# A two-layer hybrid backbone: GpSimd's products, sums, differences and copies on VectorE

## The chip, the cores and the metric

One core of one Trainium2 chip. The time is device time in microseconds (us) of one launch of the whole program. The engines in the profile are PE (TensorE, matmuls), PEld (TensorE's weight loads), DVE (VectorE), ACT (ScalarE), POOL (GpSimd) and SP (SyncE, which here issues nearly all DMAs).

## The reference

Two layers. In each, a modulated RMSNorm feeds four token mixers in parallel (gated DeltaNet, S5, differential attention, gated linear attention); their outputs are merged by sigmoid gates, multiplied by `w_out` and added to the stream; a second norm feeds a router and a mixture of experts (16 experts, two per token). Layer 0 computes 768 tokens (256 of context, 512 latent), layer 1 only what the 512 latent tokens need.

```python
def merge_branches(a, ys, w_branch, w_gate, b_gate, w_out):
    acc = 0.0
    for i, y in enumerate(ys):
        gate = jax.nn.sigmoid(a @ w_gate[:, i * dm:(i + 1) * dm] + b_gate[i * dm:(i + 1) * dm])
        acc = acc + gate * (y.astype(a.dtype) @ w_branch[i])
    return acc @ w_out

def moe_ffn(h, w_router, b_router, w_e_gate, w_e_up, w_e_down):
    scores = jax.nn.sigmoid((h @ w_router).astype(F32))
    ...                       # two experts per token, tokens sorted into blocks of 128
    def expert_block(args):
        rows, e = args
        hid = jax.nn.silu(rows @ w_e_gate[e]) * (rows @ w_e_up[e])
        return hid @ w_e_down[e]
```

## The kernel before

Activations lie in SBUF with 128 channels or 128 tokens on the partitions. Every large fp32 product is made of three TensorE matmuls (`mm3`): each operand is split into a high part `hi` that TensorE's fp32r format holds exactly and a rest `lo = raw - hi`; the product is hi·hi + lo·hi + hi·lo. So each weight tile costs one DMA (`raw`, `wr`), one ScalarE copy that rounds (`hi`, `wh`) and one subtraction (`lo`, `wl`). `wunit` makes a split for projections, gates, merge and `w_out`; `unit` makes one for the experts (six tiles of 128x2048 per expert, j = 0 to 5: two of gate, up and down each).

The program order of a layer: norm and projections; the mixers (DeltaNet, linear attention, attention head by head, S5), while the gate matmuls `pg` (L1299 to L1301 with `ah` and `al`; 1536 in layer 0) fill TensorE's gaps; the tables of the next layer's S5 (`s5_tables`, lines 1030 to 1130, with the small matmuls `s_w` and `s_h`) at the end of layer 0's mixers; the merge (`pb`, then `t`, L1765 to L1772); the product with `w_out` (`po`), the second norm and the router; the routing (lines 1966 to 2165), which ends in `tokfirst`, the list of tokens of the first block; then the experts: `front` gathers a block's rows with an indirect DMA on GpSimd's queue (`x`, L2220), transposes them on TensorE (`pt`) and splits them (`xh`, `xl`); `gate_up` and `down` are matmuls `pg`, `ph`, `pd`; an indirect DMA scatters the result (L2264). After layer 1 the pairs are added and normed.

GpSimd makes a part of the elementwise work: the `wl` of every gate tile (`pool_lo=True`), one in three `lo` of the experts (j = 2 and 5; of each layer's first expert j = 0, 1, 2 and 5, `FIRST_LO`), three of the four adds per output block of the merge, half of the S5 tables, and products in the mixers and norms. The tile framework's scheduler simulates the program when it is built, and the order of instructions on each engine follows from that simulation. An engine runs its own list strictly in that order, and each instruction waits by semaphores for what it reads and overwrites. The experts' `raw` tiles lie in a ring, and a later tile is loaded when the `hi` and `lo` of an earlier one are done.

Of the kernel before, what the change touches and what calls it, by code (L numbers as in the profile page):

```python
# [7 lines left out]
F32 = mybir.dt.float32  # L8
# [3 lines left out]
OP = mybir.AluOpType  # L12
# [11 lines left out]
AFTER = (1, 2, 5)  # L24
# [13 lines left out]
FIRST_LO = (0, 1, 2, 5)  # L38
# [319 lines left out]
def dn_pair(K, l, pr, S, qT, kT, vT, o_out, need):  # L358
# [68 lines left out]
    for d, m in ((0, "mskf"), (1, "mskb")):  # L427
        nc.gpsimd.tensor_mul(Dm[:, 12 * d:12 * d + 12], Dm[:, 12 * d:12 * d + 12],
                             K.c(m)[:, None, :].to_broadcast([128, 12, 64]))
# [89 lines left out]
    for d in range(2):  # L519
        nc.gpsimd.tensor_mul(Rk[:, d], Kb, eG[:, pr, d].rearrange("p t h -> p (t h)")[:, :, None].to_broadcast([128, 12, 64]))  # L520
    for d in range(2):
        nc.gpsimd.tensor_mul(kd[:, d], Kb, wk[:, d].rearrange("p t h -> p (t h)")[:, :, None].to_broadcast([128, 12, 64]))
# [21 lines left out]
    nc.gpsimd.tensor_mul(Mt.rearrange("p s h e -> p (s h) e"), K.c("id64")[:, None, :].to_broadcast([128, 24, 64]),  # L544
# [45 lines left out]
    for h in range(2):  # L590
        nc.gpsimd.tensor_copy(qs[64 * h:64 * h + 64], qT[64 - 64 * h:128 - 64 * h])
    Ev = EG.rearrange("p (t h) i -> p t h i", h=2)
    for d in range(2):
        dr = slice(64 * d, 64 * d + 64)
        for h in range(2):
            for t0, t1 in ((0, 2), (2, 6)):
                if t0 >= T0:
                    c0 = tcol(t0)
                    q_ = (qT if d == h else qs)[dr, c0:c0 + (t1 - t0) * 128].rearrange("p (t i) -> p t i", i=128)
                    (nc.gpsimd if d else nc.vector).tensor_mul(Ev[dr, t0:t1, h], Ev[dr, t0:t1, h], q_)  # L600
# [42 lines left out]
def finish_heads(K, pool, tag, o, tiles, eps, gain, z=None, rq=None, sq=None, head=None):  # L643
# [20 lines left out]
    if z is None:  # L664
        nc.gpsimd.tensor_mul(ov, ov, gb)
        return
# [4 lines left out]
    nc.gpsimd.tensor_mul(th, th, gb)  # L671
# [15 lines left out]
def gla(K, l, qT, kT, lowT, vsrc, need):  # L687
# [56 lines left out]
    nc.gpsimd.tensor_mul(kd, bf, kT[:, None, :].to_broadcast([128, 2, 768]))  # L744
# [63 lines left out]
def diff_attn(K, l, qk, V, o, with_ctx, done):  # L808
# [16 lines left out]
    for t in range(2, NT):  # L825
# [11 lines left out]
    def prep(h, st):  # L837
# [3 lines left out]
        for i in range(4):  # L841
# [7 lines left out]
            nc.gpsimd.tensor_sub(lo, src, sp[:, a:, 0, :].bitcast(F32))  # L849
# [180 lines left out]
def s5_tables(K, l, P, h, td):  # L1030

    nc, p, I = K.nc, K.s5, K.I
    V, G = nc.vector, nc.gpsimd
# [41 lines left out]
    G.memset(Bd, 0.0)  # L1075
# [48 lines left out]
    G.memset(dec[:, :, :, 0:1], 0.0)  # L1124
# [10 lines left out]
def s5_half(K, l, td, h, ud, zd):  # L1135
# [3 lines left out]
    V, G = nc.vector, nc.gpsimd  # L1139
# [22 lines left out]
    for d in range(2):  # L1162
# [26 lines left out]
        G.memset(x[:, :, :, first:first + 1], 0.0)  # L1189
# [86 lines left out]
def wunit(K, ring, src, shape, bufs, raw_bufs=2, pool_lo=False, tag="w", scale=None, raw_tag=None):  # L1276
# [61 lines left out]
def norm_a(K, l, md, tile_of, ah, al):  # L1338
# [56 lines left out]
    def block(s, t0, t1, k):  # L1395
# [8 lines left out]
        (nc.vector if k % 3 == 2 else nc.gpsimd).tensor_sub(al[:, k, c], v[:, 0:n], ah[:, k, c].bitcast(F32))  # L1404
# [85 lines left out]
def mixers(K, l, md, hold, tile_of, yd, gd, tds):  # L1490
# [243 lines left out]
def merge(K, l, md, hsrc, yd, gd, h1d, fd, lg, R, side):  # L1734
# [15 lines left out]
    for oc in range(8):  # L1750
# [79 lines left out]
    def product(t):  # L1830
# [7 lines left out]
        for n in range(2):  # L1838
# [4 lines left out]
            (nc.gpsimd if n == 0 else nc.vector).tensor_add(h[:, cc], h[:, cc], u[:, cc])  # L1843
# [28 lines left out]
    def tails(ss, *ts):  # L1872
# [6 lines left out]
        for i, (t, h, ps) in enumerate(ts):  # L1879
            s = 1 if t < 2 else 0  # L1880
            a, b = h[:, 0:512], h[:, 512:D]
            if t < NT - 2:
                nc.scalar.activation(a, a, AF.Copy, scale=r[:, i:i + 1])
                nc.gpsimd.tensor_mul(a, a, rows["sc", s][:, 0:512])
            else:
                nc.vector.scalar_tensor_tensor(a, a, r[:, i:i + 1], rows["sc", s][:, 0:512], op0=OP.mult, op1=OP.mult)
            nc.gpsimd.tensor_add(a, a, rows["sh", s][:, 0:512])
# [76 lines left out]
def route(K, l, lg, R):  # L1964
# [16 lines left out]
    V, G = nc.vector, nc.gpsimd  # L1981
# [18 lines left out]
    G.memset(pre[:, 0], 0.0)  # L2000
# [128 lines left out]
    G.memset(R.ent, 0)  # L2129
# [39 lines left out]
def moe(K, l, fd, metad, R, pd, ra, na, routing, rest):  # L2169
# [21 lines left out]
    def unit(e, j, alone=False, pool_lo=None, after=None):  # L2191
# [12 lines left out]
        with tc.issue_after(after.ins) if after else contextlib.nullcontext():  # L2204
            (nc.gpsimd if (j % 3 == 2 if pool_lo is None else pool_lo) else nc.vector).tensor_sub(l_, r, h.bitcast(F32))  # L2205
        return hi, lo

    def front(c, src):
# [3 lines left out]
        else:  # L2212
# [3 lines left out]
            nc.gpsimd.tensor_scalar(wt, mt[:, 2:3].bitcast(F32), 0.5, None, op0=OP.mult)  # L2216
# [50 lines left out]
    def run(work, first=False):  # L2267
# [7 lines left out]
        for i, (e, ranked, _) in enumerate([(w[0], len(w) > 2, 0) for w in work]):  # L2275
            if ranked:
                e = nc.values_load(R.exps[0:1, e:e + 1], min_val=0, max_val=13, engines=[mybir.EngineType.SP])
            us = [unit(e, j, pool_lo=j in FIRST_LO if first and i == 0 else None,
                       after=gathers[0] if first and i == 0 and j in AFTER else None, **kw) for j in range(4)]
            nxt = [front(*x) for x in work[i + 1][1]] if i + 1 < len(work) else None  # L2280
            hds = gate_up(frs, us)
            us = [unit(e, j, pool_lo=j in FIRST_LO if first and i == 0 else None,
                       after=gathers[0] if first and i == 0 and j in AFTER else None, **kw) for j in range(4, 6)]
# [32 lines left out]
def combine(K, l, md, p, h, t, rows, pd):  # L2316
# [7 lines left out]
    for i, e in ((0, nc.gpsimd), (1, nc.vector)):  # L2324
# [147 lines left out]
```

## Time and profile before

| | |
|---|---|
| time, median of 3 runs | 2811.99 us (2797.94 to 2814.32) |
| profiled execution | 2812.61 us, span of the trace 2810.6 us |
| PE busy | 2443.4 us (87%) |
| DVE busy | 1870.6 us (67%), 3515 instructions |
| ACT busy | 1218.6 us (43%) |
| POOL busy | 1178.3 us (42%), 854 instructions |
| DMA | 534.95 MB, mean 190 GB/s |
| mean granted TensorE clock | 0.908 |

The span is one launch on the core, 2 us less than the time of the same execution. A busy share is a share of the span; the engines work beside each other, so the shares don't add up to one.

### The profile page before, as it was taken

What the parts mean: (1) busy time and instruction counts of PE and PEld (TensorE: products, weight loads), DVE (VectorE), ACT (ScalarE), POOL (GpSimd) and SP (SyncE); (2) the same over time, 40 slices, a digit from 0 to 9 for tenths busy, and PEclk for the clock granted to TensorE, in tenths of its full rate; (3) what the DMA queues carried; (4) which work ended last, traced back from release to release, by engine and by line L of the source; (5) the groups of instructions that cost most, each with busy time, mean ns of one, the idle gap of its engine ahead of it and who ended that gap; (6) DMA issues with size and microseconds to landing.
All of it is one profiled execution on the core that took longest, in us unless ns stands there. A gap on an engine that the chain in (4) does not pass through costs nothing. (4 is left out here: it accounts for less than half of the span.)

```text
span 2810.6 us, 46335 instructions
## 1 busy us (share of the span) xinstructions
PE 2443.4 (87%) x17539; PEld 1974.6 (70%) x17539; DVE 1870.6 (67%) x3515; ACT 1218.6 (43%) x1889; POOL 1178.3 (42%) x854
## 2 busy tenths in 40 slices
PE   6789998899998788599998499989998886699993
PEld 5567687777776676478887388977776665478782
DVE  5968639545659765877775744665584576787775
ACT  4121232365443322366665323244655432366672
POOL 2701205522417453466664320155343043576763
PEclk9889999999988999699999699989998598799996
DMA  7488832414322775478887553343432184588884
GB/s 295 163 260 287 263 91 74 145 58 143 113 82 95 266 228 201 178 271 307 305 306 253 209 186 116 100 130 120 113 102 62 57 263 170 196 335 298 305 309 160
DMA packets 227896, 534.95 MB, mean 190 GB/s; under 512 B 85478, under 2 KB 108230, under 8 KB 202054
## 3 DMA queue, kind: packets, MB, share of 16 engines
q1 hardware_dynamic: 216710, 510.81, 53.5%
q0 software_dynamic: 10944, 20.99, 2.1%
q8 instruction: 142, 2.33, 0.3%
q14 instruction: 100, 0.82, 0.1%
HBM read 452.33 MB, written 100.35 MB: 197 GB/s over the span
## 5 line engine op out<-in xcount | busy, mean ns | idle before, releaser
L2205 DVE TENSOR_TENSOR lo<-raw,hi 128x2048 fp32r<-128x2048 f32 x124 | 418.2, 3381 | 106.3 <-ACT hi L2203 106.1
L2203 ACT ACTIVATE hi<-raw 128x2048 fp32r<-128x2048 f32 x192 | 364.2, 1913 | 79.3 <-issue 34.8
L2205 POOL TENSOR_TENSOR lo<-raw,hi 128x2048 fp32r<-128x2048 f32 x68 | 335.9, 4941 | 142.0 <-ACT hi L2203 127.5
L1290 POOL TENSOR_TENSOR wl<-wr,wh 128x512 fp32r<-128x512 f32 x128 | 185.0, 1449 | 295.5 <-ACT wh L1289 276.2
L1301 PE MATMUL pg<-ah,wl 128*128 128x512 f32 (+1 forms) x768 | 286.4, 374 | 7.1 <-POOL wl L1290 7.1
L1299 PE MATMUL pg<-ah,wh 128*128 128x512 f32 (+1 forms) x768 | 286.8, 374 | 5.8 <-ACT wh L1289 3.7
L1300 PE MATMUL pg<-al,wh 128*128 128x512 f32 (+1 forms) x768 | 286.4, 373 | 0.0
L1300 PE MATMUL pg<-lo,xh 128*128 128x512 f32 x608 | 244.9, 403 | 13.8 <-DVE lo L2205 11.0
L1299 PE MATMUL pg<-hi,xh 128*128 128x512 f32 x608 | 243.8, 404 | 5.4 <-ACT xh L2230 4.0
L1301 PE MATMUL pg<-hi,xl 128*128 128x512 f32 x608 | 243.0, 401 | 0.0
L1289 ACT ACTIVATE wh<-wr 128x512 fp32r<-128x512 f32 (+3 forms) x208 | 147.8, 715 | 206.9 <-PE pg L1300 66.8
L1301 PEld LDWEIGHTS pg<-ah,wl 128*128 128x128 f32 x768 | 151.9, 198 | 31.1 <-POOL wl L1290 8.0
L1299 PEld LDWEIGHTS pg<-ah,wh 128*128 128x128 f32 x768 | 152.1, 198 | 28.7 <-ACT wh L1289 4.2
L1300 PEld LDWEIGHTS pg<-al,wh 128*128 128x128 f32 x768 | 152.0, 198 | 22.8 <-issue 0.2
L1300 PE MATMUL pt<-wl,ah 128*128 128x256 f32 (+1 forms) x544 | 159.0, 293 | 2.2 <-DVE wl L1290 2.2
L1299 PE MATMUL pt<-wh,ah 128*128 128x256 f32 (+1 forms) x544 | 158.4, 292 | 2.3 <-ACT zst L1578 2.3
L1301 PE MATMUL pt<-wh,al 128*128 128x256 f32 (+1 forms) x544 | 157.6, 290 | 0.0
L870 DVE TENSOR_REDUCE nm<-da_m 128x1 f32<-128x384 f32 (+1 forms) x144 | 76.2, 539 | 120.0 <-PE da_m L869 118.9
L1300 PEld LDWEIGHTS pg<-lo,xh 128*128 128x128 f32 x608 | 116.9, 192 | 42.0 <-DVE lo L2205 14.4
L1299 PEld LDWEIGHTS pg<-hi,xh 128*128 128x128 f32 x608 | 117.2, 193 | 29.9 <-ACT xh L2230 5.1
L1301 PEld LDWEIGHTS pg<-hi,xl 128*128 128x128 f32 x608 | 116.8, 192 | 23.2
L1299 PE MATMUL pd<-hi,hh 128*128 128x512 f32 x304 | 120.6, 397 | 7.3 <-ACT hh L2257 4.2
(735 smaller groups left out, 6172.1 us busy)
## 6 DMA issues: line engine op xcount, KB each, us to landing
raw<-in_w_e_gate SPq DMA_DIRECT2D x64, 1024.0 KB
raw<-in_w_e_up SPq DMA_DIRECT2D x64, 1024.0 KB
raw<-in_w_e_down SPq DMA_DIRECT2D x64, 1024.0 KB
w<-in_wm SPq DMA_DIRECT2D x80, 512.0 KB
wr<-in_w_gate SPq DMA_DIRECT2D x128, 256.0 KB
wr<-in_win SPq DMA_DIRECT2D x40, 512.0 KB
gd<-gst SPq DMA_DIRECT2D x32, 384.0 KB
g<-gd SPq DMA_DIRECT2D x32, 384.0 KB
```

The lines of the kernel that those rows point to most:

```text
L870: nc.vector.tensor_reduce(nm[:, g, m, qt:qt + 1], ps[:, 0:k1 - k0], axis=AX.X, op=OP.max, negate=True)
L1289: nc.scalar.activation(h, r, AF.Copy)
L1290: (nc.gpsimd if pool_lo else nc.vector).tensor_sub(l, r, h.bitcast(F32))
L1299: nc.tensor.matmul(out, ah, bh, start=(i == 0), stop=False)
L1300: nc.tensor.matmul(out, ah, bl, start=False, stop=False)
L1301: nc.tensor.matmul(out, al, bh, start=False, stop=(i == n - 1))
L2203: nc.scalar.activation(h, r, AF.Copy)
L2205: (nc.gpsimd if (j % 3 == 2 if pool_lo is None else pool_lo) else nc.vector).tensor_sub(l_, r, h.bitcast(F32))
```

## The change

All 638 elementwise instructions of GpSimd become VectorE instructions of the same shape. The gathers, the scatters and the memsets stay on GpSimd. `FIRST_LO` and `pool_lo` go. The core of the diff (the places left out are of the same kind, one `nc.gpsimd` that becomes `nc.vector`, in the mixers, norms and the final step):

```diff
-FIRST_LO = (0, 1, 2, 5)
...
 def s5_tables(K, l, P, h, td):
-    V, G = nc.vector, nc.gpsimd
+    V, G = nc.vector, nc.vector
...
-    G.memset(Bd, 0.0)
+    nc.gpsimd.memset(Bd, 0.0)
...
-def wunit(K, ring, src, shape, bufs, raw_bufs=2, pool_lo=False, tag="w", scale=None, raw_tag=None):
+def wunit(K, ring, src, shape, bufs, raw_bufs=2, tag="w", scale=None, raw_tag=None):
...
-        (nc.gpsimd if pool_lo else nc.vector).tensor_sub(l, r, h.bitcast(F32))
+        nc.vector.tensor_sub(l, r, h.bitcast(F32))
...
-        nc.gpsimd.tensor_add(a, a, b)
+        nc.vector.tensor_add(a, a, b)
         nc.vector.tensor_add(c, c, d)
-        nc.gpsimd.tensor_add(a, a, c)
+        nc.vector.tensor_add(a, a, c)
         nc.scalar.activation(ah[:, oc], a, AF.Copy)
-        nc.gpsimd.tensor_sub(al[:, oc], a, ah[:, oc].bitcast(F32))
+        nc.vector.tensor_sub(al[:, oc], a, ah[:, oc].bitcast(F32))
...
-            (nc.gpsimd if (j % 3 == 2 if pool_lo is None else pool_lo) else nc.vector).tensor_sub(l_, r, h.bitcast(F32))
+            nc.vector.tensor_sub(l_, r, h.bitcast(F32))
...
-            us = [unit(e, j, pool_lo=j in FIRST_LO if first and i == 0 else None,
-                       after=gathers[0] if first and i == 0 and j in AFTER else None, **kw) for j in range(4)]
+            us = [unit(e, j, after=gathers[0] if first and i == 0 and j in AFTER else None, **kw) for j in range(4)]
```

The scheduler orders all engines anew. Line numbers after the change are one lower from line 38 on.

**Place 1.** VectorE in the routing of layer 0, before. `hot` is what TensorE's `ent` needs, `tokfirst` what the first gather waits for, `lo` is the experts' split.

```order
L2014 TENSOR_TENSOR hot<-iota,q 128x768
L2032 TENSOR_REDUCE po<-tmp 128x12
L2043 TENSOR_SCALAR wh<-w 128x12
L2133 COPY ent<-w 128x6 x2
L2058 TENSOR_TENSOR hot_12223<-iota,po 128x768
L2058 TENSOR_TENSOR hot_12224<-iota,po 128x768
L2047 TENSOR_TENSOR wx<-wh,seltot 128x12
L2121 TENSOR_SCALAR po<-po 128x12
L2048 TENSOR_TENSOR w_12138<-wx 128x6
L2024 TENSOR_SCALAR pr_12120<-ent 128x1
L2025 TENSOR_TENSOR tokfirst<-ent,pr_12120 128x1
L2026 SCALAR_TENSOR_TENSOR pairfirst<-ent,pr_12120 128x1
```

The same place after, from four rows behind `hot` on; the first `lo` stands right behind `hot`.

```order
L2132 COPY ent<-w 128x6 x2
L2204 TENSOR_TENSOR lo<-raw,hi 128x2048
L2057 TENSOR_TENSOR hot_12223<-iota,po 128x768
L2057 TENSOR_TENSOR hot_12224<-iota,po 128x768
L2046 TENSOR_TENSOR wx<-wh,seltot 128x12
L2204 TENSOR_TENSOR lo<-raw,hi 128x2048
L2023 TENSOR_SCALAR pr_12120<-ent 128x1
L2204 TENSOR_TENSOR lo<-raw,hi 128x2048 x2
L2120 TENSOR_SCALAR po<-po 128x12
L2047 TENSOR_TENSOR w_12138<-wx 128x6
L2204 TENSOR_TENSOR lo<-raw,hi 128x2048
L2024 TENSOR_TENSOR tokfirst<-ent,pr_12120 128x1
```

All six `lo` of the first expert now stand ahead of `tokfirst` on VectorE; before, none did, and four of the six were on GpSimd, where one stood ahead of the first gather. In layer 1 four `lo` stand ahead of `tokfirst` after the change.

**Place 2.** TensorE at the end of layer 0's mixers, before: the last rows ahead of the merge's first `pb`.

```order
L1300 MATMUL pg<-al,wh 128x512
L1301 MATMUL pg<-ah,wl 128x512
L1299 MATMUL pg<-ah,wh 128x512
L1300 MATMUL pg<-al,wh 128x512
L1301 MATMUL pg<-ah,wl 128x512
L1299 MATMUL pb<-yh,wh 128x256
```

The same place after.

```order
L1298 MATMUL pg<-ah,wh 128x512
L1299 MATMUL pg<-al,wh 128x512
L1300 MATMUL pg<-ah,wl 128x512
L1057 MATMUL s_w<-cb,W 128x128 x16
L1087 MATMUL s_h<-O,Bd 32x128 x16
L1057 MATMUL s_w<-cb,W 128x128 x16
L1087 MATMUL s_h<-O,Bd 32x128 x16
L1298 MATMUL pb<-yh,wh 128x256
```

The matmuls of the S5 tables now stand behind the last gate matmul and directly ahead of the merge; before, they lay among the gates, with 68 gate matmuls in a row behind the transposes `yT` that come after them. Earlier in the same list, the attention transposes `da_n` of layer 0's last head stand behind 1308 of the 1536 gate matmuls; before, behind 1213. On VectorE the table work of layer 0 now comes wholly behind the attention's last products `pe`; before, the two were mixed.

## Rows read from the trace of the kernel before

**Rows 1.** Windows: from:to, length, busy time of each engine, granted clock, DMA share, GB/s.

```profile
0.00:400.00 400.00, 338.33 (x3352) 259.45 (x3353) 281.14 (x779) 107.87 (x193) 100.93 (x128) 0.94 0.69 230
400.00:835.00 435.00, 414.14 (x3584) 336.07 (x3583) 249.11 (x559) 209.07 (x472) 153.99 (x140) 0.93 0.35 105
835.00:949.00 114.00, 91.59 (x580) 76.01 (x579) 99.29 (x349) 37.12 (x73) 70.71 (x85) 0.89 0.46 157
949.00:1037.00 88.00, 73.63 (x386) 60.15 (x386) 69.98 (x107) 27.46 (x41) 47.17 (x22) 0.97 0.76 239
1037.00:1200.00 163.00, 117.37 (x672) 94.03 (x672) 103.80 (x248) 45.02 (x55) 68.15 (x49) 0.81 0.51 189
1200.00:1500.00 300.00, 299.45 (x1419) 247.50 (x1419) 221.41 (x136) 198.25 (x179) 189.18 (x75) 1.00 0.83 299
1575.00:2243.00 668.00, 619.51 (x5295) 512.05 (x5294) 391.11 (x805) 283.45 (x571) 200.03 (x195) 0.88 0.36 107
2243.00:2310.00 67.00, 54.48 (x197) 40.49 (x196) 55.68 (x76) 26.36 (x44) 31.04 (x22) 0.88 0.82 263
2310.00:2480.00 170.00, 118.65 (x614) 92.39 (x614) 116.75 (x230) 56.82 (x58) 80.13 (x51) 0.82 0.55 206
2480.00:2750.00 270.00, 261.56 (x1213) 212.82 (x1211) 199.95 (x121) 183.21 (x161) 188.95 (x64) 0.99 0.85 310
```

**Rows 2.** PE's waits over the span: total us, times, longest.

```profile
PE pb L1299 <- DVE t L1765: 20.7, 19, 2.5
PE pt L2228 <- DVE xl L2231: 17.7, 3, 9.4
```

**Rows 3.** Line L2205, the experts' split: duration ns min/median/max, first and last start.

```profile
L2205 DVE TENSOR_TENSOR lo<-raw,hi x124: 2271/2293/11216, 1143.2 to 2754.7; 128x2048 fp32r<-128x2048 f32 x124
...
L2205 POOL TENSOR_TENSOR lo<-raw,hi x68: 4505/4626/6506, 1134.0 to 2757.2; 128x2048 fp32r<-128x2048 f32 x68
```

**Rows 4.** Groups by shape, DVE and POOL: count, busy us, mean ns, idle before.

```profile
L2205 DVE TENSOR_TENSOR lo<-raw,hi 128x2048 fp32r<-128x2048 f32 x124 | 418.2, 3381 | 106.3 <-ACT hi L2203 106.1
...
L2264 POOL DMA_INDIRECT pd<-o,pairranked x36 | 70.9, 1971 | 60.1 <-ACT o L2263 45.9 <-PE pg L1301 5.9 <-PE pt L2228 5.2
L2220 POOL DMA_INDIRECT x<-fd,tokranked x36 | 51.9, 1443 | 21.3 <-DVE wtranked L2071 12.0 <-POOL x L2219 6.8 <-issue 2.1
...
L1768 POOL TENSOR_TENSOR t<-t 128x768 f32<-128x768 f32 x8 | 17.3, 2159 | 20.0 <-DMA g<-gd 11.4 <-DVE t L1765 8.7
```

**Rows 5.** DVE's groups by shape in the merge of layer 0 (949 to 1037).

```profile
L1765 DVE SCALAR_TENSOR_TENSOR t<-g,pb 128x512 f32<-128x512 f32 x32 | 21.7, 678 | 1.3 <-PE pb L1301 1.3
...
L1769 DVE TENSOR_TENSOR t<-t 128x768 f32<-128x768 f32 x7 | 6.7, 952 | 0.0
```

**Rows 6.** Timelines of DVE, POOL and PE, routing of layer 0: start, us, instruction.

```profile
1147.98 4.27 DVE L2096 TENSOR_SCALAR over<-cnt 128x14 f32<-128x14 f32 x1
...
1146.63 14.54 POOL L2205 TENSOR_TENSOR lo<-raw,hi 128x2048 fp32r<-128x2048 f32 x3
...
1151.51 1.11 PE L2228 MATMUL pt<-cb,x 128*128 128x128 f32 x4 [5.67 <-DMA x<-fd,tokfirst]
...
1162.75 1.12 PE L2228 MATMUL pt<-cb,x 128*128 128x128 f32 x4 [7.79 <-DVE xl L2231]
```

**Rows 7.** The same of layer 1.

```profile
2390.04 11.22 DVE L2205 TENSOR_TENSOR lo<-raw,hi 128x2048 fp32r<-128x2048 f32 x1
...
2390.12 8.97 POOL L2205 TENSOR_TENSOR lo<-raw,hi 128x2048 fp32r<-128x2048 f32 x2
...
2406.13 1.12 PE L2228 MATMUL pt<-cb,x 128*128 128x128 f32 x4 [9.36 <-DVE xl L2231]
```

**Rows 8.** Timelines of DVE and PE, end of layer 0's mixers.

```profile
932.09 0.48 DVE L947 TENSOR_TENSOR R<-R,f 128x128 f32<-128x128 f32 x1 [0.29 <-POOL f L940]
...
948.70 0.58 PE L1299 MATMUL pb<-yh,wh 128*128 128x256 f32 x1 [2.76 <-ACT wh L1289]
```

More of the change, by code (lines that the diff above doesn't have):

```diff
@@ L664, in finish_heads @@
     if z is None:
-        nc.gpsimd.tensor_mul(ov, ov, gb)
+        nc.vector.tensor_mul(ov, ov, gb)
         return
@@ L1123, in s5_tables @@
         G.tensor_copy(dec[:, d], r8[:, d][:, :, None].to_broadcast([128, 4, 96]))
-    G.memset(dec[:, :, :, 0:1], 0.0)
+    nc.gpsimd.memset(dec[:, :, :, 0:1], 0.0)
     c = 0
@@ L1138, in s5_half @@
     nc, p, I = K.nc, K.s5, K.I
-    V, G = nc.vector, nc.gpsimd
+    V, G = nc.vector, nc.vector
     s3, s4 = K.s5_3, K.s5_4
@@ L1188, in s5_half @@
         first = 0 if d == 0 else 31
-        G.memset(x[:, :, :, first:first + 1], 0.0)
+        nc.gpsimd.memset(x[:, :, :, first:first + 1], 0.0)
         segs = [(slice(0, 95), slice(1, 96))] if d == 0 else [(slice(0, 31), slice(30, None, -1)), (slice(31, 95), slice(95, 31, -1))]
@@ L1883, in tails @@
                 nc.scalar.activation(a, a, AF.Copy, scale=r[:, i:i + 1])
-                nc.gpsimd.tensor_mul(a, a, rows["sc", s][:, 0:512])
+                nc.vector.tensor_mul(a, a, rows["sc", s][:, 0:512])
             else:
                 nc.vector.scalar_tensor_tensor(a, a, r[:, i:i + 1], rows["sc", s][:, 0:512], op0=OP.mult, op1=OP.mult)
-            nc.gpsimd.tensor_add(a, a, rows["sh", s][:, 0:512])
+            nc.vector.tensor_add(a, a, rows["sh", s][:, 0:512])
             nc.vector.scalar_tensor_tensor(b, b, r[:, i:i + 1], rows["sc", s][:, 512:D], op0=OP.mult, op1=OP.mult)
@@ L1980, in route @@
     pp = Hold(tc, f"rtp{l}", "left", space=PSUM)
-    V, G = nc.vector, nc.gpsimd
+    V, G = nc.vector, nc.vector
     f = "p t e -> p (t e)"
@@ L1999, in route @@
     pre = tl([128, n, 16], "pre")
-    G.memset(pre[:, 0], 0.0)
+    nc.gpsimd.memset(pre[:, 0], 0.0)
     sc, sel, tot = lg[:, T0:].rearrange(f), R.sel, R.tot
@@ L2128, in route @@
     V.scalar_tensor_tensor(R.row, po, 128.0, ex, op0=OP.add, op1=OP.add)
-    G.memset(R.ent, 0)
+    nc.gpsimd.memset(R.ent, 0)
     for k in range(2):
@@ L2189, in weights, with unit @@
         return w[e] if isinstance(e, int) else w[bass.ds(e, 1)].rearrange("a h p n -> (a h) p n")
-    def unit(e, j, alone=False, pool_lo=None, after=None):
+    def unit(e, j, alone=False, after=None):
         lo = ring.tile([128, 4, 512], F32R, tag="lo", bufs=HILO, name="lo")
@@ L2277, in run @@
                 e = nc.values_load(R.exps[0:1, e:e + 1], min_val=0, max_val=13, engines=[mybir.EngineType.SP])
-            us = [unit(e, j, pool_lo=j in FIRST_LO if first and i == 0 else None,
-                       after=gathers[0] if first and i == 0 and j in AFTER else None, **kw) for j in range(4)]
+            us = [unit(e, j, after=gathers[0] if first and i == 0 and j in AFTER else None, **kw) for j in range(4)]
             nxt = [front(*x) for x in work[i + 1][1]] if i + 1 < len(work) else None
             hds = gate_up(frs, us)
-            us = [unit(e, j, pool_lo=j in FIRST_LO if first and i == 0 else None,
-                       after=gathers[0] if first and i == 0 and j in AFTER else None, **kw) for j in range(4, 6)]
+            us = [unit(e, j, after=gathers[0] if first and i == 0 and j in AFTER else None, **kw) for j in range(4, 6)]
             for fr, hd in zip(frs, hds):
@@ L2323, in combine @@
     row = rows[1 if t < 2 else 0]
-    for i, e in ((0, nc.gpsimd), (1, nc.vector)):
+    for i, e in ((0, nc.vector), (1, nc.vector)):
         c = slice(512 * i, 512 * i + 512)
```

32 lines of the change are left out of this document (16 added, 16 removed).

## The prediction

> **What bounds the kernel now.** I read the windows by stage first [rows 1]. In layer 0's experts (1200 to 1500) PE is busy 299.45 of 300 us; in layer 1's (2480 to 2750) 261.56 of 270, with DMA at 0.85. In the mixers PE is busy 414.14 of 435 (layer 0) and 619.51 of 668 (layer 1). So in 1673 of 2811 us TensorE has little to give, and an edit on VectorE and GpSimd can move the end only in the rest: the start (PE 338 of 400), the end of layer 0's mixers (91.6 of 114), the two merges (73.6 of 88, 54.5 of 67), and the two stretches from the merge to the full speed of the experts (117.4 of 163, 118.7 of 170), where 46 and 51 us of PE are idle. Then I read PE's waits [rows 2]: 17.7 us for `xl`, 20.7 us for `t`, both VectorE's. Last the pairs that run at the same time.
>
> They show the one large effect. A `lo` of 128x2048 takes VectorE 2.27 us at best, 2.29 in the median and up to 11.22 [rows 3]; the sum of 124 is 418.2 us, where 124 x 2.29 would be 284 [rows 4]. So 134 us of this line alone is delay. When: `over`, 14 numbers per partition, takes 4.27 us from 1147.98 while GpSimd makes three `lo` in a row from 1146.63 [rows 6], and the 11.22 us `lo` from 2390.04 lies beside two of GpSimd's, 8.97 us from 2390.12 [rows 7]. A VectorE instruction that works from SBUF stands still until GpSimd's elementwise instruction ends. One that reads PSUM doesn't show it: `t` from `pb` took 678 ns in the mean beside GpSimd's adds [rows 5].
>
> The Trainium skill has this as a rule in two halves (Perfetto Trace Analysis, Optimizing Scalar/DVE Operations): work of a saturated VectorE may be given to GpSimd, but as the two share a port it might not help. The trace agrees with the second half, at the 11.22 us above. By the first half alone both merges would cost their upper ends below (+12, +8) and the tables +18, and the sum would be 2839 us.
>
> **The price of what is moved.** GpSimd is busy 1178.3 us (table above). Its gathers and scatters stay, 51.9 and 70.9 us [rows 4], so at most 1055 us moves, fills still in it. On VectorE the `lo` costs 2.29 instead of 4.63 us (0.50) [rows 3], an add of 128x768 0.95 [rows 5] instead of 2.16 (0.44) [rows 4]; at 0.47 that is at most 496 us more on VectorE, against delays that end: 134 on one line, and on the others unknown, at most all 1055 us in which GpSimd worked. VectorE's sum thus stays near its 1870 us, and where it lies decides.
>
> **Stage by stage**, against the profiled execution of 2812.6 us (span 2810.6; the median of the runs is 2812.0, so the two stand for each other).
>
> *Experts, 0.* VectorE in 1200 to 1500 is busy 221; GpSimd's 189 us at 0.5 make 316 without relief, but some 50 us of the 189 are gathers and scatters (40% of 122.8), which leaves 221 + 70 = 291, and half of the 134 us of delay goes: 224. Both are under 300, and PE covers it. In layer 1 the same gives 200 + 70 - 67 = 203 of 270.
>
> *Merges, +4 and +3.* Layer 0: VectorE 70.0, GpSimd 47.2 at 0.44 = 20.8, sum 90.8 in a stage of 88. Evictions from PSUM get no relief, so I take off little, 4 us at most: 87 to 91. VectorE becomes as long as the stage, PE's 73.6 no longer covers it, and waits between the two engines come on top: +4 (0 to +12). Layer 1: 55.7 + 0.44 x 31.0 = 69.3 in 67: +3 (0 to +8).
>
> *Layer 0's mixers, +6.* Two things. The order puts 95 more gate matmuls ahead of the last head's `da_n`. At the pace of the full stage, 300 us / 1419 = 0.21 us each, that is 20 us of PE ahead of the chain that ends the mixers; PE's idle time in 400 to 835 is 435 - 414 = 21 us. If all of it is filled with them the head is not later, if none is it comes 20 us later. Behind the head come VectorE's tables, and the merge's first `pb` now stands directly behind their matmuls; before, the last table product on VectorE was at 932.09 and gates filled PE until `pb` at 948.70 [rows 8]. VectorE's work in 835 to 949 is 99.3, GpSimd's 70.7 at 0.47 is 33: 132 without relief, 18 over the 114 of the stage; if every microsecond of GpSimd had stopped VectorE, 99 - 71 + 33 = 61. The row it is nearest to is line L2205, where a third of the time was delay (134 of 418): 99 - 33 + 33 = 99. So the tables end about when they did, and there are 16 us of slack from 932.6 to 948.7. I take +6 from the heads, ends -5 and +38.
>
> *Routing and first expert of layer 0, -6.* Six `lo` go ahead of `tokfirst`: 6 x 2.29 = 13.7 us, less a standstill as that of `over` (4.3) which GpSimd's first `lo` laid on this chain too: +9. So `pt`, at 1151.51, comes at about 1161; but the `xl` that held the next `pt` until 1162.75 (7.79 us of wait) is no longer stuck behind standstills [rows 6]. Up to there +9 - 8 = about 0. What is gained comes behind: GpSimd's three `lo` were done only at 1161.2, now all six are before the gather, some 9 us sooner, and so are the loads into their `raw` tiles. Ends +5 (only the chain, and a little lost) and -14 (all 46 us of idle time less a third); I take -6.
>
> *The same of layer 1, -8.* Four `lo` ahead of `tokfirst`: 9.2 - 4.3 = +5. The `lo` of 11.22 becomes 2.29, -9, and the wait of 9.36 for `xl` goes with it [rows 7]. Alone -4; with the loads that start sooner in a stage where DMA is at 0.85 up to -14; I take -8.
>
> *Start and layer 1's mixers, 0 and -4.* At the start VectorE has 281 + 0.47 x 101 = 328 of 400 us without relief, and PE waits for both: 0 (-6 to +10). In 1575 to 2243 PE is idle 48 us; VectorE goes from 391 to between 285 (391 - 200 + 94) and 485 of 668: -4 (-15 to +8), no new queue at the end, since no tables are made there.
>
> **Sum:** +4 + 3 + 6 - 6 - 8 + 0 - 4 = -5, so 2812.6 - 5 = 2808 us. The forecast's own range is 2785 to 2835. About 1% (28 us) is what a measurement of this kernel can tell from no change: its three runs lie 16 us apart.
>
> **Rivals.**
>
> *Slower: VectorE's list becomes the end of layer 0's mixers.* No idle time is filled by the gates moved up (+20) and the tables run at the price without relief (+18); PE, its gates used up, stands before `s_w` and the merge. With both merges (+7) and half of the gains in the routings (-7) that is 2812.6 + 38 + 7 - 7 = 2850. It decides once the tables end more than 16 us behind 932.6. For it speaks the order, in which nothing is left on PE behind the tables; against it that VectorE was stopped by GpSimd in this stage as elsewhere. Chance 0.19.
>
> *Faster: relief reaches TensorE.* PE is idle 97 us in the two routings (46 + 51) and 92 in both mixers and at the tables (21 + 22 + 49). If a third of it, the share of delay in L2205, goes, that is 63, less the 14 us that the `lo` ahead of both `tokfirst` cost (9 + 5) and the merges' 7: -42, 2771. For it: the waits of [rows 2] are VectorE's. Against: the same engine now has 496 us more in its list. Chance 0.28.
>
> *Gathers late.* Of 36 gathers and 36 scatters (1.44 and 1.97 us [rows 4]) most are covered, GpSimd being idle most of the time; only the first gather and last scatter of each layer lie on the path. If each waits for one `lo` of VectorE, 4 x 2.3 = 9 us: 2817. The Trainium skill (SBUF — State Buffer, Who interferes with whom) has such a rule: VectorE copies in a two-port mode lock GpSimd out of writing descriptors. No row here shows a gather that waited so. Chance 0.03.
>
> That the change doesn't do what it says is excluded: the order has no elementwise instruction left on GpSimd.
>
> **Chances and range.** The forecast 0.50, the three rivals 0.19, 0.28 and 0.03. By their ranges: faster by over 1% 0.28, within 1% 0.53, slower 0.19. The range reaches from below the faster rival to near the slower, 2762 to 2846, leaving out the outer parts of both.
>
> **What would show it.** In the profile after: `lo` at 2.29 us in median and nearly in the maximum, `over` well under 1 us; POOL under 200 us busy; VectorE within 100 us of its 1870; PE at 99% in layer 0's experts. The merge 4 us longer with VectorE busy nearly all of it. First `pt` of layer 0 some 9 us further behind the router, the second without an 8 us wait. The first `pb` between 944 and 987: beyond 965 the slower rival has it. I am wrong if a stage in which I see PE as the bound (1200 to 1500, the mixers) changes by over 10 us, since I have no term there.

## The result, and the profile after

The changed kernel takes 2724.07 us in the median (2722.04 to 2725.65, 4 runs), the kernel before 2811.77 us in the runs beside it: ratio 0.9697, 95% interval 0.9665 to 0.9730. It is 3% faster, 88 us. The forecast was 2808 us, the range 2762 to 2846; the time lies below it.

The busy times of the engines and the number of their instructions, of the changed kernel:

```profile
span 2723.8 us, 46113 instructions
...
PE 2383.1 (87%) x17539; PEld 1937.9 (71%) x17539; DVE 1915.8 (70%) x4153; ACT 1216.0 (45%) x1889; POOL 193.1 (7%) x216
...
PEclk8989997999999599799999799998998789799997
```

VectorE has 638 instructions more and is busy 45 us more: what GpSimd gave it nearly equals what it no longer stood still. TensorE does the same 17539 matmuls and is busy 60 us *less*. That is two thirds of the gain, and the prediction had no place for it; TensorE's idle time, which it did count, fell by 27 us (367 to 341).

The windows by stage, of the changed kernel; they answer to [rows 1], with the boundaries moved to the same matmuls:

```profile
396.00:825.00 429.00, 419.29 (x3684) 347.79 (x3684) 272.67 (x696) 214.26 (x483) 8.80 (x16) 0.94 0.36 107
825.00:952.50 127.50, 75.18 (x470) 59.54 (x468) 96.06 (x436) 38.28 (x73) 1.44 (x5) 0.76 0.46 154
952.50:1039.00 86.50, 75.81 (x384) 62.23 (x384) 74.24 (x121) 22.70 (x33) 0.00 (x0) 0.94 0.70 221
1572.00:2191.00 619.00, 583.60 (x5298) 486.52 (x5299) 402.57 (x957) 281.92 (x568) 12.94 (x36) 0.93 0.38 116
2372.00:2445.00 73.00, 72.98 (x347) 59.98 (x346) 67.76 (x48) 57.08 (x49) 21.04 (x12) 1.00 0.98 384
```

Two windows of the kernel before with the boundaries of the last two (layer 1 up to its merge; the first 74 us of layer 1's experts):

```profile
1574.00:2243.00 669.00, 620.51 (x5298) 513.05 (x5299) 392.11 (x806) 284.45 (x572) 200.48 (x195) 0.88 0.36 107
2426.00:2500.00 74.00, 59.99 (x258) 47.16 (x259) 63.44 (x29) 46.52 (x39) 52.36 (x16) 0.91 0.76 285
```

Read them in pairs. Layer 1 up to its merge: 5298 matmuls in both, 669 us before and 619 after; of the 50 us, 37 are PE busy (620.5 to 583.6) and 13 idle, and the granted clock rose from 0.88 to 0.93, that is, less of the stretch was at 1.2 GHz and more at 2.4. The first stretch of layer 1's experts: TensorE does 347 matmuls instead of 258 in about the same time, DMA moves 384 instead of 285 GB/s.

The split of the experts and the two instructions of layer 0's routing, of the changed kernel; `over` took 4.27 us in [rows 6], the longest `lo` took 11216 ns in [rows 3]:

```profile
L2204 DVE TENSOR_TENSOR lo<-raw,hi x192: 2277/2285/2339, 1138.6 to 2671.1; 128x2048 fp32r<-128x2048 f32 x192
```

```profile
1154.33 0.15 DVE L2024 TENSOR_TENSOR tokfirst<-ent,pr 128x1 int32<-128x1 f32 x1
...
1155.68 0.17 DVE L2095 TENSOR_SCALAR over<-cnt 128x14 f32<-128x14 f32 x1
```

None of these stands still any more. TensorE's timeline around layer 0's merge, of the changed kernel, is the other side:

```profile
879.17 0.40 PE L1300 MATMUL pg<-ah,wl 128*128 128x512 f32 x1
...
913.06 6.72 PE L1087 MATMUL s_h<-O,Bd 128*32 128x128 f32 x32 [1.99 <-DVE Bd L1078]
952.51 0.58 PE L1298 MATMUL pb<-yh,wh 128*128 128x256 f32 x1 [32.73 <-ACT wh L1288]
```

The gates end at 879.6, 66 us sooner than before (948.70 less the wait of 2.76 in [rows 8]), and the merge still begins at 952.5; TensorE stands idle for 32.7 us. SyncE's queue there:

```profile
930.01 1.06 SPq L1130 DMA_DIRECT2D td<-R  x2
934.07 4.74 SPq L1280 DMA_DIRECT2D wr<-in_w_out  x2
938.90 0.86 SPq L1130 DMA_DIRECT2D td<-R  x2
942.75 0.33 SPq L1280 DMA_DIRECT2D wr<-in_w_out  x1
943.17 1.81 SPq L1280 DMA_DIRECT2D yr<-yd  x4
```

The merge's inputs `yr` stand in this queue behind the last table stores (`td`), which come with VectorE's last table products, and behind one more load of `w_out`, issued 3 us after them.

Where the time went (87 us between the two traces), from the starts of the first and last `pb`, the first `na` and the last `pd` of each layer in the two timelines: up to layer 0's merge +4, merge -2, from its last `pb` to the last `pd` (router, routing and experts) -11, to layer 1's first `na` +7, layer 1 up to its merge -50, its merge -2, from there to the last `pd` -32, rest -1.

### The profile page after: what moved, and what is told of

It reads as the page before. It is cut to its first block, busy times and chain, and to the rows that moved or that the text cites. A ratio compares the mean times of both kernels' runs of the same rounds, so it can differ in the third digit from the quotient of the medians.

```text
span 2723.8 us, 46113 instructions
## 1 busy us (share of the span) xinstructions
PE 2383.1 (87%) x17539; PEld 1937.9 (71%) x17539; DVE 1915.8 (70%) x4153; ACT 1216.0 (45%) x1889; POOL 193.1 (7%) x216
## 5 line engine op out<-in xcount | busy, mean ns | idle before, releaser
L2204 DVE TENSOR_TENSOR lo<-raw,hi 128x2048 fp32r<-128x2048 f32 x192 | 437.2, 2287 | 84.1 <-ACT hi L2202 82.3
L1298 PE MATMUL pg<-ah,wh 128*128 128x512 f32 (+1 forms) x768 | 278.7, 363 | 4.8 <-ACT gst L1724 4.8
L1300 PE MATMUL pg<-ah,wl 128*128 128x512 f32 (+1 forms) x768 | 277.5, 362 | 2.5 <-DVE wl L1289 2.5
L1299 PE MATMUL pg<-al,wh 128*128 128x512 f32 (+1 forms) x768 | 278.0, 362 | 0.0
L1289 DVE TENSOR_TENSOR wl<-wr,wh 128x512 fp32r<-128x512 f32 (+3 forms) x208 | 164.3, 792 | 118.5 <-ACT wh L1288 117.0
L1298 PEld LDWEIGHTS pg<-ah,wh 128*128 128x128 f32 x768 | 146.2, 190 | 26.7 <-ACT gst L1724 5.7
L1300 PEld LDWEIGHTS pg<-ah,wl 128*128 128x128 f32 x768 | 146.0, 190 | 24.3 <-DVE wl L1289 3.0
L1299 PEld LDWEIGHTS pg<-al,wh 128*128 128x128 f32 x768 | 146.1, 190 | 21.1
L1298 PE MATMUL pc<-ah,wh 128*128 128x512 f32 (+3 forms) x352 | 121.0, 345 | 0.8 <-ACT ust L1536 0.7
L1299 PE MATMUL pc<-al,wh 128*128 128x512 f32 (+3 forms) x352 | 120.5, 343 | 0.0
```

Source lines behind the costliest of these rows:

```text
L1289: nc.vector.tensor_sub(l, r, h.bitcast(F32))
L1298: nc.tensor.matmul(out, ah, bh, start=(i == 0), stop=False)
L1299: nc.tensor.matmul(out, ah, bl, start=False, stop=False)
L1300: nc.tensor.matmul(out, al, bh, start=False, stop=(i == n - 1))
L2204: nc.vector.tensor_sub(l_, r, h.bitcast(F32))
```

## The experiments

Theory 1, *standstill*: VectorE's instructions from SBUF stand still while GpSimd computes, and that is what was removed. Theory 2, *order*: the scheduler happened to find a better order. Theory 3, *latency*: GpSimd's results came late, because it is slow, and what it does to VectorE doesn't matter. All ratios are to the kernel before on the same chip. The table has the stages of each profiled run, in us, from the starts of matmuls in the timelines: start to the first `pb`; last `pb` to last `pd` of layer 0 (routing and experts); first `na` to first `pb` of layer 1; last `pb` to last `pd` of layer 1.

| run | to merge 0 | experts 0 | layer 1 to merge | experts 1 | span | ratio |
|---|---|---|---|---|---|---|
| before | 949 | 502 | 669 | 460 | 2811 | 1 |
| after | 953 | 491 | 619 | 428 | 2724 | 0.970 |
| after_again | 935 | 490 | 620 | 432 | 2710 | 0.970 |
| b_moe | 950 | 492 | 678 | 430 | 2779 | 0.989 |
| b_gate | 952 | 503 | 627 | 472 | 2787 | 0.990 |
| b_gm | 940 | 493 | 656 | 432 | 2762 | 0.984 |
| a_moe | 946 | 500 | 630 | 456 | 2766 | 0.984 |
| a_gate | 952 | 493 | 640 | 431 | 2750 | 0.979 |
| a_both | 951 | 501 | 660 | 469 | 2810 | 0.999 |
| a_tab | 949 | 492 | 631 | 436 | 2746 | 0.971 |
| a_lock | 946 | 507 | 616 | 449 | 2751 | 0.981 |
| a_fill | 947 | 494 | 628 | 433 | 2732 | 0.972 |
| a_junk256 | 945 | 571 | 626 | 512 | 2893 | 1.033 |
| a_tok | 955 | 492 | 651 | 429 | 2751 | 0.978 |
| a_ord2 | 942 | 494 | 634 | 435 | 2738 | 0.973 |
| a_ord3 | 940 | 493 | 624 | 433 | 2720 | 0.974 |
| b_ord2 | 952 | 508 | 687 | 477 | 2857 | 1.015 |
| a_glock | 957 | 493 | 647 | 429 | 2756 | 0.982 |

The ratio comes from several executions, the stages from one. The runs after and after_again are one program in one order, and up to layer 0's merge they differ by 17 us, so a smaller difference in that column says nothing. The granted clock shows where most of it came from; 400 to 500 us, first after, then after_again:

```profile
400.00:500.00 100.00, 97.77 (x656) 84.48 (x655) 60.02 (x139) 34.37 (x53) 7.94 (x10) 0.78 0.33 86
400.00:500.00 100.00, 97.95 (x732) 84.69 (x731) 71.04 (x162) 38.85 (x63) 7.95 (x10) 0.91 0.38 107
```

TensorE is busy 98% of the time in both and gets through 656 matmuls in the one, 732 in the other.

### The parts, done or undone alone

b_moe: the kernel before with the experts' split on VectorE.

```diff
-            (nc.gpsimd if (j % 3 == 2 if pool_lo is None else pool_lo) else nc.vector).tensor_sub(l_, r, h.bitcast(F32))
+            nc.vector.tensor_sub(l_, r, h.bitcast(F32))
```

> The kernel before, with every `lo` of the experts on VectorE and all else as it was. Theory 1, standstill (VectorE's instructions from SBUF stand still while GpSimd computes, and what the experts gained is that they no longer do): between the two traces the stretch from the first to the last `pd` fell from 351.6 to 336.3 us in layer 0 and from 341.9 to 310.0 in layer 1, so 2812 - 47 = 2765 (2755 to 2778). Theory 2, order (the scheduler's new order of the whole program made the gain, and a part alone doesn't have it): 2812 within 12. Theory 3, latency (a `lo` takes 4.6 us on GpSimd and 2.3 on VectorE, and only that counts, not what it does to VectorE): the same 2765 as theory 1.

Measured 0.9888 (0.9835 to 0.9941), 2780.83 us. The experts became 10 and 30 us shorter, as in the change; 9 us went back in layer 1 up to its merge, in which no `lo` stands, with another order there. So the time lies 3 us above the range of theories 1 and 3 and 19 us below that of theory 2; the sum over both expert stages (some 40 us) is near the 47 that the first two had. The first 74 us of its layer 1 experts look like those of the changed kernel:

```profile
2432.00:2506.00 74.00, 72.56 (x343) 59.72 (x342) 67.55 (x48) 59.18 (x50) 19.98 (x12) 1.00 0.96 380
```

b_gate: the kernel before with the gates' `wl` on VectorE.

```diff
-                               [128, 4, 128], 3, pool_lo=True)
+                               [128, 4, 128], 3)
```

> The kernel before, with the `wl` of the gates on VectorE and all else as it was (the 128 instructions of 1449 ns go to VectorE at about 680). Theory 1: layer 1 from the first `na` to the first `pb` fell from 669.2 to 619.3 us; the gates are the largest single part of GpSimd's work there, so about half of that and something in layer 0: 2812 - 25 = 2787 (2772 to 2800). Theory 2: 2812 within 12. Theory 3: nearly nothing, since TensorE waited only 7.1 us for `wl`: 2805 within 8.

Measured 0.9903 (0.9870 to 0.9936), 2785.29 us: layer 1 up to its merge 42 us shorter, its experts 12 us longer. Theory 3 had 2805 for it, since TensorE hardly waits for `wl`, and theory 2 no gain; the time fits theory 1. The stage doesn't show it as clearly: b_gm, next, has the same division of work in that stretch and another order, and took 656 us there instead of 627.

b_gm: both of these edits. a_moe, a_gate, a_both: the changed kernel with the experts' split, the gates' split, or both, back on GpSimd.

> The kernel before with both large parts on VectorE, the experts' `lo` and the gates' `wl`, and the rest of GpSimd's work where it was. Alone they gave 1.1% and 1.0%. If each part gives its own (theory 1), together about 2.1%, ratio 0.979 (0.973 to 0.984), and the last 0.9% of the change is in the small rest: norms, S5, merge adds, mixers. If the two overlap (one wait that either of them removes): 0.988.

> The changed kernel with the experts' split as it was before (one in three `lo`, and four of each layer's first expert, on GpSimd). Theory 1 and theory 3: the 47 us of the experts come back, 2724 + 47 = 2771 (2758 to 2780). Theory 2: 2724 within 12.

> The changed kernel with the gates' `wl` on GpSimd as before. Theory 1: layer 1's mixers lose what the kernel before with only this part moved had gained (34 us up to layer 1's first `pb`): 2724 + 32 = 2756 (2742 to 2770). Theory 2: 2724 within 12. Theory 3: 2724 + 5, since TensorE hardly waited for `wl`.

> The changed kernel with both large parts back on GpSimd, so that only the small rest (some 400 us of GpSimd's time) is moved. Theory 1, each part its own: ratio to the kernel before 0.991 (0.986 to 0.996). If the rest gains nothing by itself, 1.00; if VectorE with more work loses, over 1.00.

Measured b_gm 0.9835 (0.9782 to 0.9887), a_moe 0.9843 (0.9796 to 0.9891), a_gate 0.9786 (0.9746 to 0.9826), a_both 0.9994 (0.9965 to 1.0023). The experts are the clean part: in the eleven runs of the table with all `lo` on VectorE and no subtraction added beside them, routing and experts take 490 to 494 and 428 to 436 us; in the five with a third of the `lo` on GpSimd 500 to 508 and 456 to 477. The rest alone gives nothing, against the expected 0.9%; on top of the two large parts it gives 1.4%. So the parts don't add up. Most of the 1.4% lies in one stage: from b_gm to after_again layer 1 up to its merge falls from 656 to 620 us, and by b_gate's 627 in the same stretch most of that can be order.

### Standstill without moved work

a_lock: the changed kernel, with work on GpSimd that no one waits for. The scheduler kept the order of the other engines up to layer 0's routing; behind it, it moved single rows, so the recorded sentence on the order holds only for the first part.

```diff
+        with tc.issue_after(gathers[-1].ins):
+            for q in range(4):
+                g = ring.tile([128, 6, 128], mybir.dt.bfloat16, tag="junk", bufs=1, name="junk")
+                nc.gpsimd.tensor_sub(g, K.c("id")[:, None, :].to_broadcast([128, 6, 128]), K.c("id")[:, None, :].to_broadcast([128, 6, 128]))
```

> The changed kernel, with four subtractions of 128x768 on GpSimd behind each of the 38 gathers; they read a constant and write a scratch tile that nobody reads, so no buffer is held and nobody waits for a result. The order on TensorE, VectorE, ScalarE and SyncE is that of the changed kernel. About 38 x 4 x 2 = 300 us more GpSimd work in the experts. Theory 1, standstill: `lo` on VectorE goes from 2.29 to 2.6 us or more in the mean, and part of the experts' 47 us is lost (the pieces are half as long as a `lo` was on GpSimd): 2724 + 20 = 2744 (2733 to 2765). Theory 3, latency (only GpSimd's slowness on the way of data counts): 2724 within 6. Theory 2, order: 2724 within 6.

a_fill, the control: 24 fills in place of the four subtractions.

```diff
+            for q in range(24):
+                g = ring.tile([128, 256], F32, tag="junk", bufs=1, name="junk")
+                nc.gpsimd.memset(g, 0.0)
```

> The control to the run before: behind each gather 24 fills of 128x256 of the scratch tile instead, which read nothing; about 38 x 24 x 0.3 = 270 us more GpSimd work, the same order on the other engines. Theory 1, if it is reading that makes VectorE stand still: 2724 within 6. If the loss in the run before comes from gathers and scatters that stand behind the added work in GpSimd's list: the same loss here.

Measured a_lock 0.9808 (0.9749 to 0.9867), a_fill 0.9719 (0.9668 to 0.9771), that is, 2751.85 and 2735.25 us on the same chip: a_lock inside theory 1's range, a_fill 5 us above the one it was given, with the changed kernel's 0.970 inside its interval. The groups by shape, first of a_lock, then of a_fill:

```profile
L2204 DVE TENSOR_TENSOR lo<-raw,hi 128x2048 fp32r<-128x2048 f32 x192 | 528.6, 2774 | 52.7 <-ACT hi L2202 51.8
...
L2225 POOL TENSOR_TENSOR junk<-cb 128x768 bf16<-128x768 f32 x152 | 377.4, 2483 | 9.4
```

```profile
L2204 DVE TENSOR_TENSOR lo<-raw,hi 128x2048 fp32r<-128x2048 f32 x192 | 437.6, 2287 | 93.7 <-ACT hi L2202 92.0
...
L2225 POOL MEMSET junk<- 128x256 f32 x912 | 286.1, 314 | 49.4
```

With GpSimd's subtractions in the program the `lo` take 2774 ns in the mean, with its fills 2287. In a_lock the 113 that overlap a subtraction in time take 3117 ns and the other 79 take 2283; in a_fill the 104 that overlap a fill take 2287. Routing and experts take 507 and 449 us with the one, 14 and 17 more than the middle of the eleven runs (493 and 432), and 494 and 433 with the other. Nobody waits for the added results and no buffer of the program is held by them, so theory 3 can't explain a_lock; and as fills that stand in the same place of GpSimd's list (286 us of them against 377) cost nothing there, it isn't the wait of gathers behind added work. It goes the other way too: GpSimd's subtraction of 128x768 took 1462 ns at least and 2714 in the median:

```profile
L2225 POOL TENSOR_TENSOR junk<-cb x152: 1462/2714/3516, 1150.0 to 2657.6; 128x768 bf16<-128x768 f32 x152
```

a_junk256 was a first attempt at this, and a bad one.

```diff
+        if j % 3 == 2:
+            hf = h.bitcast(F32)
+            for q in range(8):
+                g = ring.tile([128, 256], F32, tag="junk", bufs=1, name="junk")
+                nc.gpsimd.tensor_sub(g, hf[:, 256 * q:256 * q + 256], hf[:, 256 * q:256 * q + 256])
```

> The changed kernel, and for every third `lo` (which stays on VectorE) GpSimd also subtracts the same `hi` tile from itself, in eight pieces of 128x256, into a tile that nobody reads; about 64 x 5 = 320 us more GpSimd work in the experts, no work taken from VectorE and none waited for except GpSimd's own gathers and scatters behind it. Theory 1: VectorE's `lo` are stretched to 3 us and more in the mean and the experts lose what they had gained, 2724 + 40 = 2764 (2745 to 2775). Theory 3: 2724 within 8. Theory 2: 2724 within 12.

Measured 1.0328 (1.0281 to 1.0375), 2902.17 us, 127 us above the highest time that any theory allowed, and with `lo` on VectorE at 2405 ns in the mean instead of the 3 us and more that theory 1 had. ScalarE's waits show why:

```profile
ACT hi L2202 <- POOL junk L2209: 201.0, 24, 13.1
```

The added reads hold the `hi` tiles, and ScalarE waits 201 us for them. That is a ring of buffers behind a slow reader, not a standstill, so the time says nothing on theory 1. Its forecast for `lo` failed all the same: pieces of 128x256 lengthen it by 5% only.

### The order

a_tok: an edge that puts five of the first expert's `lo` behind `tokfirst` (place 1 of the change).

```diff
-AFTER = (1, 2, 5)
+AFTER = (1, 2, 3, 4, 5)
...
-            us = [unit(e, j, after=gathers[0] if first and i == 0 and j in AFTER else None, **kw) for j in range(4)]
+            us = [unit(e, j, after=R.firstins if first and i == 0 and j in AFTER else None, **kw) for j in range(4)]
...
```

> The changed kernel with an edge that puts the `lo` of the first expert, all but j = 0, behind `tokfirst` on VectorE in both layers. Up to there the order on all engines is that of the changed kernel. In the changed kernel the first `pt` of layer 0 came 10.8 us later than before. If the six `lo` ahead of `tokfirst` cost what the prediction said, the gather comes some 10 us sooner in layer 0 and 5 in layer 1, of which the later `lo` give a part back: 8 us less than the changed kernel (3 to 14). If the loads of the experts' weights set that stretch, the same as the changed kernel within 3.

Measured 0.9784 (0.9728 to 0.9840), slower than the changed kernel on the same chip by 32 us (2749.77 against 2717.59). In layer 0 the edge did what it should and gained nothing: the first `pt` came 15.6 us behind `pos` (the routing's matmuls of positions) instead of 26.2, but the last `pd` 392 us behind it in both, and in the first 75 us from `pos` on TensorE did 331 matmuls in a_tok and 334 in after_again. The 32 us are elsewhere: layer 1 up to its merge took 651 instead of 620 us, in another order.

a_ord2, a_ord3 and b_ord2 draw that order anew by exchanging two experts, which leaves the work of every engine as it was. This is the edit of a_ord2 and b_ord2, with the second half of the line left out; a_ord3 exchanges the eighth and ninth:

```diff
-ORDER = ((4, 0, 5, 6, 1, 7, 8, 2, 9, 10, 3, 11, 12, 13),
+ORDER = ((4, 0, 5, 6, 1, 7, 8, 2, 9, 10, 11, 3, 12, 13),
```

> The changed kernel with two experts of layer 0 in the other order (the eleventh and twelfth of fourteen), which makes the scheduler order layer 0's last experts and all of layer 1 anew, with the same work on every engine. Theory 1, standstill: the stretch of layer 1 from the first `na` to the first `pb` stays at 620 us within 8, the total at 0.970 within 0.004. Theory 2, order: it lies anywhere from 620 to 665, as in the runs so far.

> The same with another pair of experts (the eighth and ninth): a second draw of the order. Theory 1: 620 within 8. Theory 2: anywhere from 620 to 665.

> The kernel before with the experts of a_ord2 exchanged: a second draw of its order. Theory 1: that stretch stays at 669 within 8, ratio 1.000 within 0.004. Theory 2: anywhere from 620 to 680.

Measured 0.9728 (0.9684 to 0.9772), 0.9737 (0.9685 to 0.9790), 1.0153 (1.0104 to 1.0203). In layer 1 up to its merge they took 634, 624 and 687 us. So the order alone moves this stretch by up to 18 us in these three, and the kernel before by 44 us as a whole; theory 1's 620 and 669 "within 8" hold in one of the three. The largest moves at equal work in that stretch are those of a_tok (31 us above after_again) and of b_gm (some 30 above b_gate).

a_glock brings GpSimd's work back beside the gates and takes none from VectorE; `echo` is a scratch tile that only the gates' splits have and nobody reads.

```diff
+        if echo is not None:
+            nc.gpsimd.tensor_sub(echo, h.bitcast(F32), h.bitcast(F32))
```

> The changed kernel, and for each `wl` of the gates (which stays on VectorE) GpSimd also subtracts `wh` from itself into a scratch tile that nobody reads: GpSimd's 185 us of the gates are back beside VectorE's work in both layers' mixers, and no data waits for them but the ring of `wh`. Theory 1: layer 1 up to the merge becomes 640 us or more, ratio 0.980 (0.975 to 0.988). Theory 2: within what a_ord2 and a_ord3 show.

Measured 0.9822 (0.9771 to 0.9873), and 647 us in layer 1 up to its merge:

```profile
1581.00:2228.00 647.00, 597.77 (x5299) 494.62 (x5298) 431.69 (x954) 281.75 (x567) 96.04 (x97) 0.90 0.36 110
```

VectorE is busy 432 us there instead of 403 with the same work, and `wl` of 128x512 takes 772 ns in the mean instead of 686, so the standstill is real in the mixers too. Its price in time isn't settled: 647 is what theory 1 had (640 or more) and more than a_ord2 and a_ord3 show, but a_tok took 651 with 13 us of GpSimd's work there instead of 96. GpSimd's copies of the work also read `wh`, and ScalarE waits for them, but only 5.6 us in all.

a_tab: the changed kernel with half of the S5 tables' work back on GpSimd.

```diff
-    V, G = nc.vector, nc.vector
+    V, G = nc.vector, nc.gpsimd
```

> The changed kernel with half of the S5 tables' work on GpSimd as before. After the change TensorE stands idle for 32.7 us ahead of layer 0's merge, behind the tables. If VectorE's list sets that end (the slower rival of the prediction, hidden by gains elsewhere), two engines make the tables sooner and the merge comes 8 to 20 us earlier: 2712 (2702 to 2718). Theory 1: the two engines stop each other, so that nothing is gained: 2724 within 6.

Measured 0.9712 (0.9665 to 0.9759): the same as the changed kernel. The merge began at 949 us, between the 935 and 953 of two executions of the changed kernel. As far as executions that differ so much can tell, two engines make the tables no sooner.

after_again is the changed kernel once more, beside b_gm, a_both and a_tok:

> The changed kernel once more, on the chip of this call, as the other side of the three runs above: ratio to the kernel before 0.970 (0.966 to 0.974).

Measured 0.9698 (0.9643 to 0.9754), as the first time. No version that was run is faster than the changed kernel.

## Why the prediction was wrong, step by step

**The mechanism was right and its reach was not.** The standstill was seen and priced on one line (134 us of the `lo`), and of the rivals "relief reaches TensorE" at 2771 us comes nearest. But it counted TensorE's idle time alone, and of that 27 us went, not 42. The step that failed first is the first one: that in 1673 us, where PE was busy 93 to nearly 100% of the time, "TensorE has little to give". The sum had -4 for layer 1's mixers; the trace has -50, where the prediction called 10 us in such a stage the sign that it was wrong. PE was busy 620.5 of 669 us and gave 37 us of that busy time, besides 13 of idle time.

The 37 us are the granted clock, as the matmuls are the same. By 0.88 and 0.93 about 160 us of the stretch were at 1.2 GHz before (2 x 0.12 x 669) and 87 after (2 x 0.07 x 619); half of the difference is 37. Nearly half of the 160 us is one piece at the end of the stretch. The first line is the time ahead of it, the second the piece, both before; the third is the same piece in a_junk256, that is, with the change:

```profile
2125.50:2159.60 34.10, 29.51 (x543) 22.85 (x543) 22.12 (x61) 21.82 (x55) 9.23 (x12) 1.00 0.13 41
2159.60:2234.70 75.10, 70.84 (x616) 51.12 (x618) 38.35 (x115) 35.67 (x84) 4.61 (x5) 0.50 0.00 1
2187.40:2262.50 75.10, 69.92 (x607) 50.32 (x602) 38.69 (x119) 35.26 (x83) 0.32 (x1) 0.50 0.00 1
```

In the piece before, TensorE was busy 70.8 of 75.1 us and GpSimd 4.6, so standstill can hardly act there. The changed kernel's own order has no piece as long in four executions (41 us at most), and five other orders of it have one: 58 to 75 us in a_ord3, a_ord2, a_moe, a_tok and a_junk256. So that this piece is missing is luck of the order, and not all of the 37 us is the change's. That short waits for VectorE lower the clock isn't shown either: a_tok and b_gate have 42 and 44 us of idle time in the stretch, at clocks of 0.88 and 0.93.

How much of the 50 us is standstill, how much is order, is only bounded. The three orders of the kernel before's division of work in the mixers (before, b_ord2, b_moe) took 669, 687 and 678 us. The ten executions that leave that division as the change has it (after, after_again, a_lock and a_fill in one order, and a_ord2, a_ord3, a_moe, a_junk256, a_tab and a_tok in six others) took 616 to 651, with 627 in the middle. They don't overlap, so the change has a gain apart from the draw, some 50 us from middle to middle, 18 at least between the nearest two. Its share by part is not resolved: with the gates' `wl` alone on VectorE the stretch took 627 and 656 us (b_gate, b_gm), with all but them 640 and 660 (a_gate, a_both), and 647 in a_glock lies inside the spread of the ten. Whether the rest is standstill or results that came late stays open.

**Routing and experts: -6 and -8 predicted, -11 and -32 measured.** I had PE at 99.8% of 1200 to 1500 as covering everything. That holds for the middle of the stage, not for its start: in layer 1 the first 74 us had PE at 81% and DMA at 0.76 of its time. With the `lo` on VectorE DMA moves 384 GB/s there and PE no longer waits; that the `raw` tiles come back sooner is the reading. I put -8 for that; b_moe has it as -30 alone, a_moe as +28 when undone. The step was right in kind and a quarter of the size. a_lock shows that standstill by itself costs as much as was gained in layer 0 (14 us against 11) and half of it in layer 1 (17 of 32), with pieces half as long as a `lo` was; whether the other half in layer 1 is the longer pieces or GpSimd's own 4.6 us per `lo` wasn't separated.

**Merges: +4 and +3 predicted, -2 and -2 measured.** "Evictions from PSUM get no relief, so I take off little, 4 us at most" was wrong by the other lines of the same stage. One line of the merge before, not among the rows that I had read, then the same line after:

```profile
L1287 DVE SCALAR_TENSOR_TENSOR wl<-wr,wh 128x512 fp32r<-128x512 f32 x15 | 17.6, 1176 | 7.7 <-ACT wh L1286 7.6
```

```profile
L1286 DVE SCALAR_TENSOR_TENSOR wl<-wr,wh 128x512 fp32r<-128x512 f32 x7 | 4.8, 690 | 2.1 <-ACT wh L1285 2.0
```

VectorE was busy 74.2 us in the stage, not 87 to 91: part of the `wl` had gone ahead of the merge (7 are left in it, of 15), and those take 690 instead of 1176 ns.

**Layer 0's mixers: +6 predicted, +4 measured, and that agreement is luck.** after_again, the same program, has -14 there. The slower rival's order took place: the gates ended 66 us sooner and TensorE stood before the merge, 32.7 us in one piece, but VectorE's last table product ended at 939, 6 us later than before and not the 16 from which that rival would decide:

```profile
938.76 0.29 DVE L947 TENSOR_TENSOR R<-R,f 128x128 f32<-128x128 f32 x1
```

a_tab gives no sign that VectorE's having to make all tables alone sets the end, as that rival said.

**Place 1 cost what was said, and it didn't matter.** The first `pt` of layer 0 came 26.2 us behind `pos` instead of 18.1, 8 us later (predicted +9); in layer 1 21.7 instead of 13.8, also 8 (predicted +5). a_tok takes this away and gets nothing back, so the term +9 wasn't on the path. The rule of the Trainium skill in the rival on late gathers (SBUF — State Buffer, Who interferes with whom) shows no loss to speak of here: after the change the 36 gathers take 1527 ns in the mean, where [rows 4] have 1443, and the 36 scatters 1743 instead of 1971.

```profile
L2263 POOL DMA_INDIRECT pd<-o,pairranked x36 | 62.8, 1743 | 269.3 <-ACT o L2262 267.1 <-issue 1.9 <-ACT hi L2202 0.3
L2219 POOL DMA_INDIRECT x<-fd,tokranked x36 | 55.0, 1527 | 31.2 <-DVE ovb L2157 11.1 <-DVE wtranked L2070 10.7 <-POOL x L2218 7.9
```

**Without a term.** From layer 0's last `pd` to layer 1's first `na` the change loses 7 us. The prediction has no term for that stretch, and no run separates what causes it.

## What to carry to other kernels

Work on GpSimd isn't free because GpSimd is idle: where VectorE works from SBUF at the same time, compare the mean with the lowest time of every one of its forms, and count the difference as a cost of GpSimd. Here that held for GpSimd's elementwise work, not for its fills. A TensorE that is busy 93% of a stage isn't a bound as long as its granted clock there is under 1: look at the clock beside the busy share before calling a stage covered, and don't credit a change with a better clock before several orders and executions show it. Where a scheduler orders the program, a change that does nothing can move a stage by 20 to 30 us; draw the order anew a few times before a smaller difference is believed.

## What was not expected of the hardware

GpSimd's fills didn't stop VectorE: 912 of them, 286 us, beside `lo` whose longest took 2295 ns (a_fill):

```profile
L2204 DVE TENSOR_TENSOR lo<-raw,hi x192: 2277/2286/2295, 1132.9 to 2680.4; 128x2048 fp32r<-128x2048 f32 x192
```

And small pieces on GpSimd lost to VectorE rather than stopped it: in a_junk256 subtractions of 128x256 took 602 ns at least and 2757 at most, while VectorE's `lo` took 2405 ns in the mean and never more than 2751:

```profile
L2209 POOL TENSOR_TENSOR junk<-hi x512: 602/614/2757, 1128.3 to 2853.3; 128x256 f32<-128x256 f32 x171
...
L2204 DVE TENSOR_TENSOR lo<-raw,hi x192: 2272/2291/2751, 1130.5 to 2837.2; 128x2048 fp32r<-128x2048 f32 x192
```
